# Late right-hand operands of a seven-product output projection loaded whole, row splits in one piece, and sums on GpSimd

## The chip, the cores and the metric

The kernel runs on one core of a Trainium2 chip. The metric is the time of one execution in microseconds (us), as the device reports it; lower is better. The kernel before the change took 889.74 us (median of three runs, 889.66 to 891.19).

A core has five engines with instruction queues of their own: TensorE (PE) multiplies matrices, VectorE (DVE) and ScalarE (ACT) work on rows of 128 partitions, GpSimd (POOL) and SyncE (SP) mostly issue DMAs. Each engine works through its queue in order, so an instruction that waits holds all that stand behind it on the same engine. DMAs are issued from the queues of SP, ACT and POOL.

## What is computed

The reference is one decoder block on 512 tokens of width 1024. Two mixers run on the normed input (a gated linear attention and a state-space layer), are merged by gates, projected by `w_out`, normed and added to the input; then a squared-ReLU feed-forward layer (FFN) with norms ahead of it and behind.

```python
mixed = jax.nn.sigmoid(z_gla) * y_gla + jax.nn.sigmoid(z_ssm) * y_ssm
h = h + rmsnorm(mixed @ w_out[l], g_mix_post[l])
hn = rmsnorm(h, g_ffn_pre[l])
f = jnp.square(jax.nn.relu(hn @ w_ff1[l])) @ w_ff2[l]
h = h + rmsnorm(f, g_ffn_post[l])
```

All is float32. `rmsnorm(x, g)` is `x * rsqrt(mean(x*x) + 1e-6) * g`.

## The kernel before

One function, `hybrid_block`, holds the whole block; 13,462 instructions. A float32 matrix is split into a high part (`hi`, rounded by ACT in `split_hi`, L160) and a low part (`lo = x - hi`, by VectorE), and a product of two matrices is three matmuls: hi·hi, hi·lo and lo·hi (in the names: `whi`, `wlo`, `hh`, `hl`, `gh`, `gl`, `bh`, `bl`). The order on each engine is made by a scheduler from the code and from hints: `with tc.issue_after(x)` puts what it holds behind instruction `x` in the order.

**Gated stage** (L1409 to L1489). The state-space output is loaded as eight tiles `qi` in POOL's queue (L1417) and split into `gh` and `gl`; products with `w_glu` give gate and value, two tiles of each in every one of four rounds (`c4`). In each round `out_load` (L1425) brings two 128-row blocks of `w_out` (1 MB, tile `woraw`, POOL's queue), and `out_weights` (L1430) makes from them a part of the operands of the output projection: three of the right-hand operands are split at once (`b1`, `b2_`, `b5_`), three sums `t2`, `t3`, `t4` are stored to device memory (`tdo`). `mixed` (L1443) makes the left-hand operands `ah`, `al` from the mixture tile `ms`.

**Output projection** (L1509 to L1629). The 512 x 1024 result is formed as a 2 x 2 block product by seven products instead of eight, on sums of blocks, named A11, A12, S1, S2, S4, S3, A22 in the order in which they run. Each (`out_product`, L1520) covers two token tiles `t` of 128 rows with 4 k-blocks of three matmuls 128x512: 12 matmuls to a tile, 24 to a product, summed in the PSUM banks `Xo`, `Yo`, `Zo`. The four late right-hand operands are b6 (for S2), b3 (S4), b7 (S3) and b4 (A22). `later_b` (L1527) fetches each in two loads of 512 KB from SP's queue into `wraw`, a ring of three buffers that the FFN's weights use too, and splits it in two pieces of 128x1024.

While products run, results of the finished ones are put together to rows: `out_half` (L1552) takes the squares of a half row tile on ACT and multiplies by `gpost`; `h_rows` (L1558) takes the root (`root`, L133: a Sqrt on ACT, small steps on VectorE, L140 to L147), adds the input rows `xt`, stores `h` (POOL's queue, L1567), takes the second root and scales the rows to `hn`. Rows 0 and 1 (the tiles with `t < 2`) come from the first products; rows 2 and 3 need A22. `turn_rows` (L1573) transposes `hn` by eight TensorE transposes for a row tile and splits it into `hh` and `hl`, a 128x128 piece at a time, multiplying by the gain `g_ffn_pre`, which here stands by column in `vecs`.

**First FFN tiles** (L1631 to L1643). Four weight tiles of `w_ff1` (`ws`; the fourth is `kept_w`) are multiplied with the first 256 tokens of `hh` and `hl` (24 matmuls 128x256 to a tile); the turns of rows 2 and 3 stand between them in PE's queue. After them come the second halves and the rest of the FFN.

Of the kernel before, what the change touches and what calls it, by code (L numbers as in the profile page):

```python
# [10 lines left out]
F32R = mybir.dt.float32r  # L11
# [6 lines left out]
P = 128  # L18
D = 1024
# [31 lines left out]
def hybrid_block(ctx: ExitStack, tc: tile.TileContext, io, out: bass.AP):  # L51
# [74 lines left out]
    vecs = mk(cst, [P, 44], tag="vecs")  # L126
    V_GN, V_BGLU, V_BGATE, V_D, V_GF = 0, 8, 24, 28, 36
# [31 lines left out]
    def split_hi(dst, src, scale=1.0):  # L159
        S.activation(dst, src, AF.Copy, scale=scale)  # L160
# [1251 lines left out]
    for m in range(KT):  # L1412
        if m == NBLK - 1:
            q = blocks[m].qT
        else:
            q = mk(pgl, [P, SEQ], tag="qi", bufs=4)
            nc.gpsimd.dma_start(q, qd[m])  # L1417
        split_hi(gh[:, m], q)
        V.tensor_sub(gl[:, m], q, f32(gh)[:, m])  # L1419

    def split_to(hi, lo, src):
        split_hi(hi, src)
        return V.tensor_sub(lo, src, f32(hi))  # L1423
# [36 lines left out]
    for c4, c in enumerate(range(0, D, 256)):  # L1460
        ss_ = []
        for i, w in enumerate(load_w(wg[:, D + c : D + c + 256])):
            m = c // P + i
            ps = bank("mm")
            feat_tile(w, gh, gl, 0, SEQ, ps)
            s_ = mk(pgl, [P, SEQ], tag="ms", bufs=2)
            S.activation(s_, ps, AF.Sigmoid, bias=vecs[:, V_BGLU + 8 + m : V_BGLU + 9 + m])
            zt = mk(pgl, [P, SEQ], tag="zi", bufs=2)
            nc.sync.dma_start(zt, zs[m])
            gated = V.tensor_mul(s_, s_, zt)  # L1470
            ss_.append(s_)
        with tc.issue_after(gated.ins):
            raw = out_load(c4)
            if c4 == 3:
                out_weights(c4, raw)
        for i, w in enumerate(load_w(wg[:, c : c + 256])):
            m = c // P + i
            ps = bank("mm")
            feat_tile(w, gh, gl, 0, SEQ, ps)
            t = mk(pgl, [P, SEQ], tag="ti", bufs=2)  # L1480
            nc.sync.dma_start(t, td[m])
            V.scalar_tensor_tensor(ss_[i], ps, vecs[:, V_BGLU + m : V_BGLU + m + 1], ss_[i], op0=ALU.add, op1=ALU.mult)
            added = V.tensor_add(ss_[i], ss_[i], t)
            mixed.even = ss_[0].rearrange("p (h t) -> p h t", h=2)
            mixed(c4, i, ss_[i])
        if c4 < 3:
            with tc.issue_after(added.ins):
                out_weights(c4, raw)
# [20 lines left out]
    sf = ExitStack()  # L1509
    pf = pool("pf", stack=sf, side="right", padded=True)  # L1510
    hh = mk(pf, [P, KT, SEQ], F32R, tag="hh")
    hl = mk(pf, [P, KT, SEQ], F32R, tag="hl")
    spt = ExitStack()
    pt = pool("pt", stack=spt, side="right", padded=True)
    gpost = mk(pt, [P, D], tag="gpost")
    nc.scalar.dma_start(gpost, io["g_mix_post"][0].partition_broadcast(P))
    Yo, Xo = ([bank("mm") for _ in range(2)] for _ in range(2))
    Zo = [bank() for _ in range(2)]

    def out_product(acc, i, b, t, first=False):  # L1520

        ts_ = slice(t * P, (t + 1) * P)
        for k in range(4):
            for n, (x_, w_) in enumerate(((ah[i], b[0]), (ah[i], b[1]), (al[i], b[0]))):
                PE.matmul(acc[t], x_[:, k, ts_], w_[:, k], start=first and k == 0 and n == 0, stop=k == 3 and n == 2, skip_group_check=True)

    def later_b(src):  # L1527

        hi, lo = b_slot()
        for jj in range(2):  # L1530
            raw = mk(wp, [P, 2, 512], tag="wraw", bufs=3)
            nc.sync.dma_start(raw, src(jj))
            later_b.made = split_to(hi[:, 2 * jj : 2 * jj + 2], lo[:, 2 * jj : 2 * jj + 2], raw)
        return hi, lo

    def sums_of(i):
        return lambda jj: tdo[i, 2 * jj : 2 * jj + 2].rearrange("j p n -> p j n")

    w22_of = lambda jj: w_out.rearrange("(j k p) n -> k p j n", k=2, p=P)[1, :, 2 * jj : 2 * jj + 2, 512:]
# [7 lines left out]
    def rows_x(t):  # L1547
        xt = xts_[t] = mk(pt, [P, D], tag="xt", bufs=2)
        for i in range(2):
            nc.sync.dma_start(xt[i * CH : (i + 1) * CH], io["x"][0].rearrange("(c t) d -> t c d", t=T8)[2 * t + i])  # L1550

    def out_half(t, n, i, src=None):  # L1552
        dst = rows_[t][:, sides[n]]
        src = dst if src is None else src
        out_half.squared = squares(pt, accs[t], i, src)
        V.tensor_mul(dst, src, gpost[:, sides[n]])

    def h_rows(t):  # L1558
# [5 lines left out]
        for n in range(2):  # L1564
            V.scalar_tensor_tensor(ht[:, sides[n]], ht[:, sides[n]], rs, xt[:, sides[n]], op0=ALU.mult, op1=ALU.add)  # L1565
# [3 lines left out]
        h_rows.done = V.tensor_scalar(hn[:, :512], ht[:, :512], rs, None, op0=ALU.mult)  # L1569
        h_rows.scaled = S.activation(hn[:, 512:], ht[:, 512:], AF.Copy, scale=rs)  # L1570
        return hn

    def turn_rows(t):  # L1573

        col = slice(t * P, (t + 1) * P)
        for q in range(2):
            pv = turned_tokens(hns[t], P, q, "sm")
            for k in range(4):
                kk = 4 * q + k
                g = vecs[:, V_GF + kk : V_GF + kk + 1]  # L1580
                S.activation(hh[:, kk, col], pv[:, k], AF.Copy, scale=g)  # L1581
                V.scalar_tensor_tensor(hl[:, kk, col], pv[:, k], g, f32(hh)[:, kk, col], op0=ALU.mult, op1=ALU.subtract)  # L1582
# [8 lines left out]
    b6 = later_b(sums_of(0))  # L1591
# [5 lines left out]
    b3 = later_b(w22_of)  # L1597
    ws = load_w(w1[:, : 3 * P])
    rows_[2], rows_[3] = row_tile(), row_tile()
# [5 lines left out]
    b7 = later_b(sums_of(1))  # L1605
# [3 lines left out]
    b4 = later_b(sums_of(2))  # L1609
    for t in range(2):  # L1610
        out_product(Yo, S4, b3, t)
        with tc.issue_after(later_b.made.ins):
# [3 lines left out]
    second = h_rows.done, h_rows.scaled  # L1616
# [16 lines left out]
    kept_w = [t[:, :2].rearrange("p a (k n) -> p (a k) n", n=P) for t in b_slot()]  # L1633
    raw = raw_w(w1[:, 3 * P : EARLY * P])[1]
    with tc.issue_after(second[0].ins), tc.issue_after(second[1].ins):
        split_to(*kept_w, raw)
# [185 lines left out]
def laid_out(np, given):  # L1822
# [4 lines left out]
    rows = {"vecs": np.concatenate([a[n][0].reshape(-1, P) for n in ("gla_norm_g", "b_glu", "b_gate", "d_skip", "g_ffn_pre")]).T}  # L1827
# [13 lines left out]
_LAID = ["g_mix_pre", "g_ffn_pre", "w_gate_up", "gla_norm_g", "b_glu", "b_gate", "d_skip", "a_re", "a_im", "log_step", "b_re", "b_im", "c_re", "c_im"]  # L1841
_INS = [
    "x", "meta_tokens", "w_in", "w_o_gla", "w_glu", "w_out", "g_mix_post", "w_ff1", "w_ff2", "g_ffn_post",
# [21 lines left out]
```

## Time and profile before

| | before |
|---|---|
| Median of three runs | 889.74 us (889.66 to 891.19) |
| The profiled execution: its own time | 888.97 us |
| Its span in the trace | 887.3 us |
| Mean granted TensorE clock | 0.991 of full speed |
| DVE busy | 685.1 us (77%) |
| ACT busy | 464.4 us (52%) |
| POOL busy | 131.2 us (15%) |
| HBM traffic over the span | 210 GB/s |

One execution is profiled. In a timeline a row gives the start in us, the duration in us, the engine, the line of the kernel, the operation and `out<-in` with the tiles' names, shape and type; xN means N like it in a row, and square brackets hold the time that the engine stood idle before it, with what released it. In the list of waits a row names who waited, for whom, and then us in total, times, and the longest. In a table of windows the columns are the stretch, its length, the busy time and count of PE, PE's weight loads, DVE, ACT and POOL, the granted clock, the DMA share and GB/s. In a row of groups, busy time and the mean nanoseconds of one stand behind the bar. A DMA row ends with KB for each and us from issue to landing. A busy time is a share of the span; what a wait costs is read at the engine that bounds.

### The profile page before, as it was taken

The page shows a single profiled execution, that of the slowest core. Times are in us where ns is not written, and L with a number is a line of the kernel's source. Part 1 is how long each engine was busy: PE and PEld are TensorE (multiplying, and loading weights), DVE is VectorE, ACT ScalarE, POOL GpSimd, SP SyncE. Part 2 cuts the span into 40 slices and gives each one's busy share as a digit, 9 for nine tenths or more (in the row PEclk, how much of TensorE's full clock was granted, in tenths as well). Part 3 has the DMA queues.
Part 4 walks back from the last instruction along what each step waited for, and adds up shares of the span by engine and source line. Part 5 has one row for each costly group of instructions (what it writes and reads, how often), then busy time and mean ns, then how long its engine had stood idle before and what let it go on. Part 6 is the DMA issues. An engine that isn't in the chain of part 4 may idle for free.

```text
span 887.3 us, 13462 instructions
## 1 busy us (share of the span) xinstructions
PE 865.2 (98%) x4824; PEld 738.5 (83%) x4824; DVE 685.1 (77%) x1267; ACT 464.4 (52%) x813; POOL 131.2 (15%) x229
## 2 busy tenths in 40 slices
PE   9999999999999999999999968999999999999996
PEld 8998989898988888887888856988888888888885
DVE  7999889978778699764777768566766768688786
ACT  7676467666755455244444557533222236665763
POOL 1113112031212222240111000011211200000001
PEclk9999999999999999999999997999999999999999
DMA  9767777546365857676665764289999876865564
GB/s 316 237 219 226 203 150 175 160 114 183 104 161 135 263 142 195 194 221 226 194 221 176 227 194 160 61 315 319 309 313 344 298 277 213 295 196 191 168 211 143
DMA packets 169835, 187.41 MB, mean 211 GB/s; under 512 B 18296, under 2 KB 127000, under 8 KB 169768
## 3 DMA queue, kind: packets, MB, share of 16 engines
q1 hardware_dynamic: 147856, 115.95, 44.2%
q0 software_dynamic: 19792, 65.87, 21.6%
q10 hardware_dynamic: 2120, 4.72, 1.8%
q8 instruction: 38, 0.62, 0.3%
q14 instruction: 29, 0.24, 0.1%
HBM read 147.42 MB, written 39.09 MB: 210 GB/s over the span
## 4 chain that ended last, share of the span: by engine, by line
PE 49%; DVE 2%; ACT 2%; DMA 1%; issue 0%; DVEq 0%; ACTq 0%
PE mm L61 34%; PE sm L61 15%; DMA wraw<-tdo 1%; ACT junk L1498 1%; DVE bl L1423 0%; ACT bh L160 0%; PE sm L66 0%; DVE hl L1582 0%; DVE c L1786 0%; DVE aq L1565 0%; DVE c L1780 0%; ACT L143 0%; DVE wlo L175 0%; ACT hh L1581 0%; ACT whi L160 0%
## 5 line engine op out<-in xcount | busy, mean ns | idle before, releaser
L160 ACT ACTIVATE whi<-wraw 128x1024 fp32r<-128x1024 f32 x81 | 85.8, 1060 | 191.1 <-PE mm L61 178.0
L175 DVE TENSOR_TENSOR wlo<-wraw,whi 128x1024 fp32r<-128x1024 f32 x81 | 98.6, 1223 | 83.4 <-ACT whi L160 83.1
L61 PE MATMUL mm<-xh,whi 128*128 128x512 f32 (+2 forms) x464 | 158.9, 342 | 0.0
L61 PE MATMUL mm<-xh,wlo 128*128 128x512 f32 (+2 forms) x464 | 155.8, 336 | 0.0
L61 PE MATMUL mm<-xl,whi 128*128 128x512 f32 (+2 forms) x464 | 155.6, 335 | 0.0
L61 PE MATMUL mm<-hl,whi 128*128 128x512 f32 (+1 forms) x272 | 102.2, 376 | 2.8 <-DVE hl L1582 1.5
L61 PE MATMUL mm<-hh,whi 128*128 128x512 f32 (+1 forms) x272 | 102.4, 377 | 1.0 <-ACT hh L1581 1.0
L61 PE MATMUL mm<-hh,wlo 128*128 128x512 f32 (+1 forms) x272 | 101.8, 374 | 0.0
L61 PEld LDWEIGHTS mm<-xh,whi 128*128 128x128 f32 x464 | 87.6, 189 | 9.6 <-issue 1.0
L61 PEld LDWEIGHTS mm<-xh,wlo 128*128 128x128 f32 x464 | 87.5, 189 | 9.0
L61 PEld LDWEIGHTS mm<-xl,whi 128*128 128x128 f32 x464 | 87.7, 189 | 8.4
L1723 DVE TENSOR_TENSOR wlo<-wraw,whi 128x1024 fp32r<-128x1024 f32 x56 | 68.4, 1223 | 20.0 <-ACT whi L1719 19.7
L61 PE MATMUL sm<-wlo,fh 128*128 128x512 f32 x192 | 74.8, 390 | 0.0
L61 PE MATMUL sm<-whi,fl 128*128 128x512 f32 x192 | 74.7, 389 | 0.0
L61 PE MATMUL sm<-whi,fh 128*128 128x512 f32 x192 | 74.7, 389 | 0.0
L1719 ACT ACTIVATE whi<-wraw 128x1024 fp32r<-128x1024 f32 x56 | 58.6, 1049 | 17.2 <-PE mm L61 11.7
L61 PEld LDWEIGHTS mm<-hl,whi 128*128 128x128 f32 x272 | 52.3, 192 | 12.4 <-DVE hl L1582 2.2
L61 PEld LDWEIGHTS mm<-hh,whi 128*128 128x128 f32 x272 | 52.4, 193 | 10.5 <-ACT hh L1581 1.7
L61 PEld LDWEIGHTS mm<-hh,wlo 128*128 128x128 f32 x272 | 52.3, 192 | 8.8
L160 ACT ACTIVATE fh<-f 128x512 fp32r<-128x512 f32 x48 | 30.3, 631 | 44.1 <-PE sm L61 30.2
L61 PE MATMUL mm<-gl,whi 128*128 128x512 f32 x128 | 50.0, 391 | 1.4 <-DVE gl L1419 1.4
L61 PE MATMUL mm<-gh,whi 128*128 128x512 f32 x128 | 50.0, 391 | 0.0
(474 smaller groups left out, 1861.9 us busy)
## 6 DMA issues: line engine op xcount, KB each, us to landing
wraw<-in_w_ff_dram SPq DMA_DIRECT2D x56, 512.0 KB, 4.8
wraw<-in_w_in_dram SPq DMA_DIRECT2D x46, 512.0 KB, 4.2
w2raw<-in_w_ff_dram POOLq DMA_DIRECT2D x16, 1024.0 KB, 8.8
t2d<-w2t POOLq DMA_DIRECT2D x16, 1024.0 KB, 5.8
wraw<-t2d SPq DMA_DIRECT2D x32, 512.0 KB, 3.7
wraw<-in_w_glu_dram SPq DMA_DIRECT2D x16, 512.0 KB, 6.3
M<-kpad POOLq DMA_DIRECT2D x64, 64.0 KB, 3.1
wraw<-in_w_o_gla_dram SPq DMA_DIRECT2D x8, 512.0 KB, 6.2
```

The costliest lines, as they stand in the source:

```text
L61: ins = nc.tensor.matmul(*args, **kw)
L160: S.activation(dst, src, AF.Copy, scale=scale)
L175: V.tensor_sub(lo, raw, f32(hi))
L1498: return S.activation(junk, src, AF.Square, accum_out=acc[:, i : i + 1])
L1719: halved = S.activation(bh, raw, AF.Copy)
L1723: V.tensor_sub(bl, raw, f32(bh))
```

## The change

- **Late operands.** The four raw right-hand operands (128x4x512, 1 MB each) are loaded whole (`raw_b`) from POOL's queue into a pool `pr`, which takes the memory in which `hh` and `hl` lie later; `later_b` only splits them, in two pieces as before. The input rows of `t < 2` are loaded in POOL's queue behind them.
- **Row splits.** `g_ffn_pre` is loaded as a broadcast row (`gffn`, a second load in ACT's queue behind `gpost`) and multiplied into the rows ahead of their scaling, the first half on GpSimd and the second on VectorE. `turn_rows` then splits a half row tile in one piece on ACT (L160) and one on VectorE (L213).
- **GpSimd** takes the two sums with `p5o`, two multiplies by `gpost`, and the four first-half multiplies by `gffn`.
- **Order.** The first FFN weights are split within the end of the gated stage, the fourth ahead of the split of b4; a Sqrt on a scrap tile has the ACT table loaded behind the split of b3; the turn of row 1 is put inside A22's second tile; the first `woraw` load goes behind all `qi` loads.

In the code (cut):

```diff
-            nc.gpsimd.dma_start(q, qd[m])
+            last_q = nc.gpsimd.dma_start(q, qd[m])
...
-        with tc.issue_after(gated.ins):
+        with tc.issue_after(last_q.ins):
             raw = out_load(c4)
+        with tc.issue_after(gated.ins), tc.issue_after(opened.ins):
             if c4 == 3:
                 out_weights(c4, raw)
...
+    gffn = mk(pt, [P, D], tag="gffn")
     nc.scalar.dma_start(gpost, io["g_mix_post"][0].partition_broadcast(P))
+    nc.scalar.dma_start(gffn, io["g_ffn_pre"][0].partition_broadcast(P))
...
+    def raw_b(i, src):
+        raw = mk(pr, [P, 4, 512], tag=f"rawb{i}")
+        nc.gpsimd.dma_start(raw, src)
+        return raw
...
-    def later_b(src):
+    def later_b(raw):
         hi, lo = b_slot()
-        for jj in range(2):
-            raw = mk(wp, [P, 2, 512], tag="wraw", bufs=3)
-            nc.sync.dma_start(raw, src(jj))
-            later_b.made = split_to(hi[:, 2 * jj : 2 * jj + 2], lo[:, 2 * jj : 2 * jj + 2], raw)
+        for kk in (slice(0, 2), slice(2, 4)):
+            later_b.made = split_to(hi[:, kk], lo[:, kk], raw[:, kk])
...
-        V.tensor_mul(dst, src, gpost[:, sides[n]])
+        out_half.made = (engine or V).tensor_mul(dst, src, gpost[:, sides[n]])
...
+            (V if n else G).tensor_mul(hn[:, sides[n]], ht[:, sides[n]], gffn[:, sides[n]])
...
-        h_rows.done = V.tensor_scalar(hn[:, :512], ht[:, :512], rs, None, op0=ALU.mult)
-        h_rows.scaled = S.activation(hn[:, 512:], ht[:, 512:], AF.Copy, scale=rs)
+        V.tensor_scalar(hn[:, :512], hn[:, :512], rs, None, op0=ALU.mult)
+        S.activation(hn[:, 512:], hn[:, 512:], AF.Copy, scale=rs)
...
     def turn_rows(t):
...
-                S.activation(hh[:, kk, col], pv[:, k], AF.Copy, scale=g)
-                V.scalar_tensor_tensor(hl[:, kk, col], pv[:, k], g, f32(hh)[:, kk, col], op0=ALU.mult, op1=ALU.subtract)
+        transpose_tokens(hns[t], P, hh, hl, t * P, "sm")
...
+    with tc.issue_after(later_b.made[0].ins):
+        S.activation(warm, warm, AF.Sqrt)
+    b7 = later_b(raws_b[2])
+    kept_w = [mk(pw, [P, KT, P], F32R, tag="aq", bufs=14) for _ in range(2)]
+    with tc.issue_after(later_b.made[0].ins), tc.issue_after(later_b.made[1].ins):
+        kept_made = split_to(*kept_w, raw_w(w1[:, 3 * P : 4 * P])[1])
...
-        V.tensor_add(rows_[2 + t][:, sides[1]], rows_[2 + t][:, sides[1]], p5o[:, sides[t]])
-        out_half(2 + t, 1, 0)
+        G.tensor_add(rows_[2 + t][:, sides[1]], rows_[2 + t][:, sides[1]], p5o[:, sides[t]])
+        out_half(2 + t, 1, 0, engine=G)
...
-        out_product(Xo, A22, b4, t)
-        turn_rows(t)
+        out_product(Xo, A22, b4, t, within=(lambda: turn_rows(1)) if t else None)
+        if not t:
+            turn_rows(0)
```

The order that results on three engines follows, with the program's names (a number behind a name tells tiles of one name apart).

POOL's queue at the output projection, before the change; `tdo` is a stored sum, `hd` the stored rows `h`:

```order
L1441 DMA tdo_4751<-qi_5404 128x512
L1567 DMA hd_5509<-aq_5554 128x1024
L1567 DMA hd_5509<-aq_5556 128x1024
L1567 DMA hd_5509<-aq_5634 128x1024
L1567 DMA hd_5509<-aq_5635 128x1024
```

and after it, where `rawb_946` to `rawb_949` are the raw operands of b6, b3, b7 and b4, and `aq` and `hn` rows:

```order
L1440 DMA tdo_4751<-qi_5404 128x512
L1532 DMA rawb_946_5526<-tdo_4751 128x4x512
L1532 DMA rawb_947_5528<-in_w_out_dram 128x4x512
L1532 DMA rawb_948_5530<-tdo_4751 128x4x512
L1532 DMA rawb_949_5532<-tdo_4751 128x4x512
L1556 DMA xt_5588<-in_x_dram 64x1024 x2
L1556 DMA xt_5607<-in_x_dram 64x1024 x2
L1573 TENSOR_TENSOR hn_5739<-aq_5562,gffn_5517 128x512
L1574 DMA hd_5509<-aq_5562 128x1024
L1632 TENSOR_TENSOR aq_5634<-aq_5634,aq_5659 128x512
L1632 TENSOR_TENSOR aq_5671<-aq_5671,aq_5659 128x512
L1573 TENSOR_TENSOR hn_5786<-aq_5564,gffn_5517 128x512
```

Four operand loads and four loads of input rows have come in ahead of the row stores, and arithmetic stands between the stores.

ACT's queue from the last raw operands to the first root, before; `bh_5699` is the high part of b4, `junk` a square, `wo_r` a root:

```order
L1608 COPY aq_5556<-mm_5523 128x512
L160 ACTIVATE bh_5663<-wraw_5665 128x1024
L160 ACTIVATE bh_5663<-wraw_5669 128x1024
L160 ACTIVATE bh_5699<-wraw_5701 128x1024
L160 ACTIVATE bh_5699<-wraw_5705 128x1024
L1498 ACTIVATE junk_5722,woacc_5526<-aq_5554 128x512
L143 ACT_TABLE_LOAD
L143 ACTIVATE wo_r_5726<-woacc_5526,wo_r_5726 128x1
```

and after, where `bh_5702` is b4's and `aq_5669` the fourth FFN tile's high part:

```order
L1605 ACT_TABLE_LOAD
L1605 ACTIVATE warm_74<-warm_74 128x1
L160 ACTIVATE bh_5663<-rawb_948_5530 128x1024 x2
L160 ACTIVATE aq_5669<-wraw_5672 128x1024
L1613 COPY aq_5562<-mm_5522 128x512
L1613 COPY aq_5564<-mm_5523 128x512
L160 ACTIVATE bh_5702<-rawb_949_5532 128x1024 x2
L1498 ACTIVATE junk_5727,woacc_5534<-aq_5562 128x512
L143 ACTIVATE wo_r_5731<-woacc_5534,wo_r_5731 128x1
```

The table load has moved ahead of the splits of b7, and a split of the fourth FFN tile has come in.

DVE's queue at the end of the gated stage, before; `ms` is a mixture tile, `aq_4732` and those behind it are left-hand operands:

```order
L1482 SCALAR_TENSOR_TENSOR ms_5364<-mm_5430,vecs_86,ms_5364 128x512
L1483 TENSOR_TENSOR ms_5364<-ms_5364,ti_5455 128x512
L1423 TENSOR_TENSOR aq_4732<-ms_5364,aq_4731 128x256
L1482 SCALAR_TENSOR_TENSOR ms_5394<-mm_5461,vecs_86,ms_5394 128x512
L1483 TENSOR_TENSOR ms_5394<-ms_5394,ti_5486 128x512
L1423 TENSOR_TENSOR aq_4734<-ms_5394,aq_4733 128x256
```

and after, with `wlo` the low parts of FFN weights:

```order
L1482 SCALAR_TENSOR_TENSOR ms_5364<-mm_5430,vecs_86,ms_5364 128x512
L175 TENSOR_TENSOR wlo_5626<-wraw_5622,whi_5624 128x1024
L1483 TENSOR_TENSOR ms_5364<-ms_5364,ti_5455 128x512
L1422 TENSOR_TENSOR aq_4732<-ms_5364,aq_4731 128x256
L1482 SCALAR_TENSOR_TENSOR ms_5394<-mm_5461,vecs_86,ms_5394 128x512
L1483 TENSOR_TENSOR ms_5394<-ms_5394,ti_5486 128x512
L175 TENSOR_TENSOR wlo_5632<-wraw_5628,whi_5630 128x1024
L1422 TENSOR_TENSOR aq_4734<-ms_5394,aq_4733 128x256
```

Two splits of FFN weights now stand ahead of left-hand operands.

More of the change, by code (lines that the diff above doesn't have):

```diff
@@ L1421, in split_to @@
     def split_to(hi, lo, src):
-        split_hi(hi, src)
-        return V.tensor_sub(lo, src, f32(hi))
+        return split_hi(hi, src), V.tensor_sub(lo, src, f32(hi))
     def out_load(j):
@@ L1486, in hybrid_block @@
         if c4 < 3:
-            with tc.issue_after(added.ins):
+            with tc.issue_after(added.ins), tc.issue_after(opened.ins):
                 out_weights(c4, raw)
@@ L1608, in hybrid_block @@
         S.copy(rows_[t][:, sides[1]], Xo[t])
-    b4 = later_b(sums_of(2))
+    with tc.issue_after(kept_made[0].ins), tc.issue_after(kept_made[1].ins):
+        b4 = later_b(raws_b[3])
+    spr.close()
+    sf = ExitStack()
+    pf = pool("pf", stack=sf, side="right", padded=True)
+    hh = mk(pf, [P, KT, SEQ], F32R, tag="hh")
+    hl = mk(pf, [P, KT, SEQ], F32R, tag="hl")
     for t in range(2):
         out_product(Yo, S4, b3, t)
-        with tc.issue_after(later_b.made.ins):
+        with tc.issue_after(out_half.made.ins):
             V.tensor_add(rows_[t][:, sides[1]], rows_[t][:, sides[1]], Yo[t])
@@ L1632, in hybrid_block @@
     w2 = io["w_ff2"][0]
[L1633 to L1636, printed above, removed]
     ws.append(kept_w)
```

49 lines of the change are left out of this document (21 added, 28 removed).

## The prediction

> **What bounds the kernel now.** I read the page's table of engines first, then PE's waits, then PE's timeline where the longest of them lies.
>
> ```profile
> span 887.3 us, 13462 instructions
> PE 865.2 (98%) x4824; PEld 738.5 (83%) x4824; DVE 685.1 (77%) x1267; ACT 464.4 (52%) x813; POOL 131.2 (15%) x229
> ...
> PE mm L61 <- ACT aq L1620: 7.2, 1, 7.2
> PE mm L61 <- DVE hl L1582: 1.5, 2, 1.0
> PE mm L61 <- DVE gl L1419: 1.4, 2, 1.2
> PE mm L61 <- DVE hn_r L140: 1.3, 1, 1.3
> PE mm L61 <- ACT hh L1581: 1.0, 3, 0.4
> ```
>
> TensorE is busy 865.2 of 887.3 us, so only some 22 us of waits and the stretches at a low clock can be won. The waits are few: one of 7.2 us on the copy at L1620, 3.8 us in sum on the turned rows (L1582, L1581, and the chain behind L140), 1.4 us on gl at the start of the gated stage. The change touches just these. PE's timeline gives the stage its frame:
>
> ```profile
> 492.08 0.39 PE L61 MATMUL mm<-bh,aq 128*128 128x512 f32 x1
> ...
> 524.49 0.39 PE L61 MATMUL mm<-bh,aq 128*128 128x512 f32 x1
> 532.09 0.80 PE L61 MATMUL mm<-bh,aq 128*128 128x512 f32 x1 [7.21 <-ACT aq L1620]
> ...
> 537.13 1.04 PE L66 MATMUL sm<-ident,hn 128*128 128x128 f32 x8
> 537.92 0.47 PE L61 MATMUL mm<-bh,aq 128*128 128x512 f32 x1
> ...
> 549.20 0.41 PE L61 MATMUL mm<-hh,wlo 128*128 128x256 f32 x1
> 553.89 0.29 PE L61 MATMUL mm<-hh,whi 128*128 128x256 f32 x1
> 554.02 0.27 PE L61 MATMUL mm<-hl,whi 128*128 128x256 f32 x1
> ...
> 563.04 0.28 PE L61 MATMUL mm<-hh,bl 128*128 128x256 f32 x1
> ```
>
> The first six products (144 matmuls) run from 492.08 to 524.72: 0.227 us each, 2.72 us for one product on one tile of 128 rows, 5.44 for both. From 524.72 to the end of the four early FFN tiles (563.16, one step of 0.12 after the last row) 38.4 us pass. Undisturbed the same work takes 5.4 (A22) + 4 x 0.79 (eight transposes, 537.13 to 537.92) + 96 x 0.119 (the rows from 553.89 on) = 20.0 us. **So 18.4 us are lost there**: 7.4 before A22; 2.3 as its first half takes 5.04 us (532.09 to 537.13) instead of 2.72; about 3.8 in waits on turned rows; 2.1 as the 22 matmuls from 549.20 to 553.89 take 0.213 us each; the rest in restarts.
>
> **What the 7.2 us are.** ACT's timeline, then VectorE's:
>
> ```profile
> 522.39 1.06 ACT L160 ACTIVATE bh<-wraw 128x1024 fp32r<-128x1024 f32 x1 [1.63 <-DMA wraw<-tdo]
> 526.14 1.28 ACT L143 ACT_TABLE_LOAD   x1
> 531.47 1.04 ACT L1620 COPY aq<-mm 128x512 f32<-128x512 f32 x2
> ...
> 523.48 1.23 DVE L1423 TENSOR_TENSOR bl<-wraw,bh 128x1024 fp32r<-128x1024 f32 x1 [1.46 <-ACT bh L160]
> 524.63 1.28 DVE L1613 TENSOR_TENSOR aq<-aq,mm 128x512 f32<-128x512 f32 x2
> 528.41 1.42 DVE L1565 SCALAR_TENSOR_TENSOR aq<-aq,wors,xt 128x512 f32<-128x512 f32 x2
> 534.09 1.41 DVE L1565 SCALAR_TENSOR_TENSOR aq<-aq,wors,xt 128x512 f32<-128x512 f32 x2
> 553.09 0.48 DVE L1569 TENSOR_SCALAR hn<-aq,hnrs 128x512 f32<-128x512 f32 x1
> ```
>
> The last right-hand operand lands at 522.4. VectorE adds the rows (L1613) only behind its split, at 524.63, though the products were there long before. From that add to the end of the first copy (531.47 + 0.55 = 532.05) the chain of squares, roots and copies takes 7.4 us, 1.28 of it a table load.
>
> **The change, part by part.** (1) *Operands.* They now come as four 1 MB loads in POOL's queue. The first waits for PE's last gated product (492.08), the other three for VectorE's last read of the mixture.
>
> ```profile
> 498.11 0.42 DVE L1423 TENSOR_TENSOR aq<-ms,aq 128x256 fp32r<-128x256 f32 x1
> ...
> w2raw<-in_w_ff_dram POOLq DMA_DIRECT2D x16, 1024.0 KB, 8.8
> ...
> 576.00:586.00 10.00, 10.00 (x46) 8.29 (x45) 7.83 (x12) 2.71 (x5) 0.58 (x2) 1.00 0.88 303
> ```
>
> That read ends at 498.5, and near 499.7 with the splits put ahead of it (3). Then 3 x 1.05 MB and two broadcast vectors of 0.5 MB are 4.2 MB. No row shows three such loads in one queue. At the 303 GB/s of the window they take 13.8 us (landed 513.5); at the rate of the w2raw row, two megabytes in flight per 8.8 us (238 GB/s), 17.6 us, and issue and latency put 2 us on that (519.5). I take 516, nearer to the window's rate, since there too several queues are at work. The first load has until S2 (492.08 + 72 x 0.227 = 508.4) and is not late by either rate; the x rows, 1 MB more behind the four, come 3.5 us later, near 519.5, and are wanted at 523. Behind it stand the two ACT pieces (1.06 each, the second VectorE piece trails by one), so the add of row tile 0 begins at 516 + 1.1 + 1.2 + 1.2 = 519.5, 5.1 us earlier than now. The fourth FFN tile's split (1.06 on ACT, 1.23 on VectorE) now stands ahead of these pieces and is covered by the wait for the load; without that cover it would cost its 1.2 us.
>
> (2) *The chain from that add.* It loses the table load (1.28; ACT waits on DMA just before, so its new place is covered) and gains 0.6 (the add of row tile 1 now stands between its reciprocal and its next step) and 0.3 (gain multiply ahead of L140): 7.4 - 1.3 + 0.9 = 7.0. The copy ends at 526.5, the PE is there at 524.7: **a stall of 1.9 us instead of 7.4.** With the early landing it is 0, with the late one 5.5.
>
> (3) *Cover for the FFN splits.* Two splits of 1.23 us now stand in VectorE's queue ahead of the last left operands. Today those of A11 are ready at 492.6 and read first at 492.08 + 9 x 0.227 = 494.1 (low half 494.6).
>
> ```profile
> 492.18 0.43 DVE L1423 TENSOR_TENSOR aq<-ms,aq 128x256 fp32r<-128x256 f32 x1 [0.48 <-ACT aq L160]
> 480.08 0.72 POOL L1427 DMA_DIRECT2D woraw<-in_w_out_dram  x1
> DMA to landing us min/median/max: 5.3/5.9/10.2
> 497.77 0.35 ACTq L1516 DMA_DIRECT2D gpost<-in_g_mix_post_dram  x1
> ```
>
> At 1.23 later they still meet the low half with 0.8 us left. The weights are now issued beside the woraw load of 480.08; if they land like the slowest of that tile's answer (10.2 us) and not like its median (5.9), near 492 that is, VectorE stands up to 2 us and A11 with it. gpost is issued about 2 us later than now and holds VectorE at L1562, ahead of the first late operand's split. For both I reserve 0.9 us, between 0 and 1.8.
>
> (4) *The rows' turns.* The gain sits in hn beforehand, so a half is split by one ACT and one DVE piece of 128x512 (0.63 us, 0.68) in place of four of each (0.35 each). Row tile 0: hn is scaled some 2.6 us after its root's Sqrt, near 528.1, inside A22's first tile (526.5 to 529.3): hidden. Row tile 1 stands 5.7 us behind in the rows of L1565 now; without the two sums between (1.35, now on GpSimd) and with the multiply (0.6) 5.0, so it is scaled near 532.6; PE wants it after turn 0 and six matmuls, at 531.5: stall 1.1. Then A22 ends near 534.9; the first FFN tile waits 0.8 for its split; turn 2 waits 0.3. Row tile 3 is scaled 12.8 us after A22's end today (L1569 at 553.09 and 0.48, against 537.92 + 12 x 0.227 = 540.6); fewer pieces in between, the fourth FFN tile's split (1.06 and 1.23) among those that go, make it about 12, near 546.9, and PE is there at 544.6: stall 2.3. Waits in all: 1.9 + 1.1 + 0.8 + 0.3 + 2.3 = 6.4.
>
> (5) *The clock.* After 7.2 us the clock is halved, but also after waits on turned rows of 1.3 us at most:
>
> ```profile
> 545.00:550.00 5.00, 3.25 (x11) 2.25 (x12) 4.68 (x21) 4.08 (x14) 0.53 (x1) 0.71 0.46 166
> 550.00:555.00 5.00, 5.00 (x30) 5.00 (x29) 2.79 (x9) 2.40 (x6) 0.53 (x1) 0.61 0.26 105
> ```
>
> The new waits are as long as these but farther apart; each low stretch costs 2.1 to 2.3. I take 0.8 in all (bounds 0 and 4.4), and 0.9 for restarts. [...]
>
> So 6.4 + 0.8 + 0.9 = 8.1 stands where 18.4 stood: **the stage gains 10.3.**
>
> (6) *Start of the gated stage.* All qi loads now go ahead of woraw on POOL.
>
> ```profile
> 406.08 0.50 PE L61 MATMUL mm<-gl,whi 128*128 128x512 f32 x1 [0.23 <-DVE gl L1419]
> 408.53 0.50 PE L61 MATMUL mm<-gl,whi 128*128 128x512 f32 x1 [1.21 <-DVE gl L1419]
> 398.62 1.60 POOL L1417 DMA_DIRECT2D qi<-qd  x3
> ```
>
> The last three are issued at 398.6, behind woraw and td; two of them move up, the last one doesn't pass td. Of 1.4 us I take 0.8 (0 to 1.4).
>
> (7) *GpSimd* gets eight operations of two 128x512 inputs: four gain multiplies, two sums, two multiplies.
>
> ```profile
> L306 POOL TENSOR_SCALAR_AFFINE_SELECT sc<-sc 128x512 f32<-128x512 f32 x1 | 0.6, 633 | 0.0
> L305 POOL MEMSET sc<- 128x512 f32 x1 | 0.5, 531 | 0.1
> L160 ACT ACTIVATE fh<-f 128x512 fp32r<-128x512 f32 x48 | 30.3, 631 | 44.1 <-PE sm L61 30.2
> L175 DVE TENSOR_TENSOR wlo<-wraw,whi 128x1024 fp32r<-128x1024 f32 x81 | 98.6, 1223 | 83.4 <-ACT whi L160 83.1
> ```
>
> No two-input one is in the trace. One input takes 0.63; I take twice that, 1.3, with 0.6 (half a VectorE piece of L175, two inputs) as the lower bound; no row bounds it from above, so the upper end is where it decides. The eight and four store issues (0.7 each, as the woraw row) run in series from the first row's L1571 (523.5) until row tile 3 needs the last, at about 544: up to (544 - 523.5 - 2.8) / 8 = 2.2 us each, they hide behind VectorE's and ACT's own chain. VectorE loses eight pieces of 0.69, which the 12 us of (4) hold already.
>
> **Sum.** 10.3 + 0.8 - 0.9 = 10.2 from the profiled execution's 888.97 gives 878.8. That execution lies 0.77 under the median of 889.74, so the forecast is **879.5**.
>
> **Rivals.** *Operands late and clock down:* landing at 519.5 makes A22 wait 5.5 (3.6 more), and a wait that long halves the clock as the 7.2 did (1.5 more than taken): 884.6, with a spread to 886. For it speak the w2raw row and queue order, against it the window's 303. Chance 0.22. *Everything hides:* landing at 513.5, no clock lost, no reserve: 1.9 + 0.8 + 0.9 off, near 875.9; chance 0.11. *VectorE held by GpSimd:* if a GpSimd operation holds a two-input one of VectorE for its whole length, once in each of the three turns on the path, 3 x 1.3 = 3.9 more: 883.4. The trace has no such pair, so nothing speaks for or against; chance 0.06. [...] *It doesn't do what it says:* the operands land when they land now, since the queue was full, and the rows' chain stays late; only small terms move, 889; chance 0.06. *Slower:* GpSimd becomes the bound. Its queue ends at 526.3 + 8d, and 6.8 us of scaling, turning and matmuls follow (2.5 + 0.8 + 3.5); this passes today's 563.16 at d = 3.8. At 4.2 us the end is 566.7, 3.5 later than now, less the 0.8 of the start: 892.4. It needs over six times the one-input row, and no row shows such a factor. Chance 0.07.
>
> **How the numbers follow.** The forecast, 877 to 882.5 by its own smaller terms, has 0.48; the rivals 0.22, 0.11, 0.06, 0.06 and 0.07. Range 875.5 to 886: it takes in the two landing bounds. Faster by over 0.2% (1.8 us, about what a measurement of this kernel can tell): 0.48 + 0.22 + 0.11 + 0.06 = 0.87; same 0.06; slower 0.07.
>
> **What would show it.** Right: PE's wait on the copy of Xo falls from 7.2 to about 2 (0 to 5.5); the rawb loads land by 516; no table load behind L1624; the waits on gl at 406 to 409 shrink; GpSimd's operations take 0.6 to 2.2 us. Wrong: a new wait of A11 on a left operand near 494, of S2 on bl near 508, S4's or S3's operands late, a PE wait whose releaser is POOL, or a PEclk row that is lower through the FFN tiles than now.

## The result and the profile after

The changed kernel takes **879.66 us** (median of four runs, 879.35 to 880.48) against 890.37 us for the kernel before on the same chip (four runs): a ratio of 0.9881 with a 95% interval of 0.9864 to 0.9898, so 1.2% faster, 10.7 us. The profiled execution took 879.52 us, its span 877.6 us. Run again later, the same kernel gave 0.9885 (0.9861 to 0.9910).

The forecast was 879.5. The total agrees to 0.2 us, but its terms don't: some were too small, others too large, and they cancel. That is the subject of the rest.

The head of the page of the changed kernel, and then its list of PE's waits, in the same columns as those of before:

```profile
span 877.6 us, 13428 instructions
PE 860.9 (98%) x4824; PEld 737.3 (84%) x4824; DVE 686.8 (78%) x1243; ACT 458.0 (52%) x790; POOL 147.8 (17%) x245
```

```profile
PE sm L66 <- DVE hn L1576: 5.4, 3, 4.0
PE mm L61 <- ACT aq L1630: 1.1, 1, 1.1
```

The 7.2 us on the copy of Xo are 1.1 now, the waits on gl at the gated stage's start are gone from the list, and so are those on hh and hl. A new line has come: 5.4 us on the scaled rows (L1576), 4.0 of them at one place. PE's timeline shows where (turn n is the transposing of row tile n, the rows with L66):

```profile
490.16 0.39 PE L61 MATMUL mm<-bh,aq 128*128 128x512 f32 x1
...
522.58 0.39 PE L61 MATMUL mm<-bh,aq 128*128 128x512 f32 x1
524.07 0.50 PE L61 MATMUL mm<-bh,aq 128*128 128x512 f32 x1 [1.10 <-ACT aq L1630]
...
527.30 1.09 PE L66 MATMUL sm<-ident,hn 128*128 128x128 f32 x8 [0.22 <-DVE hn L1576]
...
533.84 1.97 PE L66 MATMUL sm<-ident,hn 128*128 128x128 f32 x8 [4.04 <-DVE hn L1576]
535.46 0.78 PE L61 MATMUL mm<-bh,aq 128*128 128x512 f32 x1
...
538.17 0.41 PE L61 MATMUL mm<-hh,whi 128*128 128x256 f32 x1
...
539.66 0.29 PE L61 MATMUL mm<-hl,whi 128*128 128x256 f32 x1
...
548.90 1.07 PE L66 MATMUL sm<-ident,hn 128*128 128x128 f32 x8 [1.13 <-DVE hn L1576]
...
553.27 0.28 PE L61 MATMUL mm<-hh,aq 128*128 128x256 f32 x1
```

A11 starts at 490.16 instead of 492.08. From the end of S3 (the row at 522.58 and 0.23, 522.81) to the end of the early FFN tiles (the row at 553.27 and 0.12, 553.39) 30.6 us pass, 7.9 less than the 38.4 before. Of these 10.6 are lost against the undisturbed 20.0: 6.5 in four waits (1.10, 0.22, 4.04, 1.13), 2.8 behind the longest of them at a low clock (0.53 granted in 535 to 540; the turn takes 1.62 us instead of 0.79, six matmuls 2.71 instead of 1.36, seven of the FFN 1.49 instead of 0.83), the rest in restarts.

What makes row 1 late stands in VectorE's timeline, beside GpSimd's:

```profile
516.48 0.68 DVE L1624 TENSOR_TENSOR aq<-aq,mm 128x512 f32<-128x512 f32 x1
...
521.23 1.68 DVE L1573 TENSOR_TENSOR hn<-aq,gffn 128x512 f32<-128x512 f32 x1
...
524.06 1.35 DVE L146 SCALAR_TENSOR_TENSOR hn_r<-hnrs,hn_r 128x1 f32<-128x1 f32 x1
525.33 0.15 DVE L145 RECIPROCAL wors<-wo_r 128x1 f32<-128x1 f32 x1
525.44 1.21 DVE L147 SCALAR_TENSOR_TENSOR hnrs<-hn_r,hnrs 128x1 f32<-128x1 f32 x1
...
528.80 1.67 DVE L1573 TENSOR_TENSOR hn<-aq,gffn 128x512 f32<-128x512 f32 x1
...
530.95 0.16 DVE L145 RECIPROCAL hnrs<-hn_r 128x1 f32<-128x1 f32 x1
531.15 1.84 DVE L146 SCALAR_TENSOR_TENSOR hn_r<-hnrs,hn_r 128x1 f32<-128x1 f32 x1
...
533.30 0.48 DVE L1576 TENSOR_SCALAR hn<-hn,hnrs 128x512 f32<-128x512 f32 x1
```

```profile
520.62 1.74 POOL L1573 TENSOR_TENSOR hn<-aq,gffn 128x512 f32<-128x512 f32 x1 [17.70 <-DVE aq L1571]
...
524.10 2.53 POOL L1632 TENSOR_TENSOR aq<-aq,aq 128x512 f32<-128x512 f32 x2 [1.20 <-ACT aq L1630]
528.18 1.74 POOL L1573 TENSOR_TENSOR hn<-aq,gffn 128x512 f32<-128x512 f32 x1 [1.55 <-DVE aq L1571]
...
530.49 2.49 POOL L1562 TENSOR_TENSOR aq<-aq,gpost 128x512 f32<-128x512 f32 x2
```

A step on 128x1 numbers (L146) takes 1.35 and 1.84 us and ends with GpSimd's operation (525.4; 532.99 against GpSimd's 532.98, the end of the second of two that follow each other); undisturbed it takes 0.22. The reciprocal beside it, with one input, takes its usual 0.15. The lengthened instructions on the way to row 1 are L1573 (1.68 and 1.67 instead of 0.69), L146 (1.35, 1.84) and L147 (1.21 instead of 0.16): 5.8 us in all.

Not each part of the gain is steady. From the first product of the gated stage to A11 the changed kernel takes 87.04 us in this execution, and so do eight of the experiments below that keep its order of loads; in e10, where it was run again, it takes 88.24, with short waits on gh (0.41) and gl (0.22).

### The profile page after: what moved, and what is told of

Its sections match the earlier page's. It is cut to its first block, busy times and chain, and to the rows that moved or that the text cites. A ratio compares the mean times of both kernels' runs of the same rounds, so it can differ in the third digit from the quotient of the medians.

```text
span 877.6 us, 13428 instructions
## 1 busy us (share of the span) xinstructions
PE 860.9 (98%) x4824; PEld 737.3 (84%) x4824; DVE 686.8 (78%) x1243; ACT 458.0 (52%) x790; POOL 147.8 (17%) x245
## 4 chain that ended last, share of the span: by engine, by line
PE 83%; DVE 6%; issue 5%; DMA 3%; ACT 2%; POOL 0%; ACTq 0%; DVEq 0%; POOLq 0%
PE mm L61 59%; PE sm L61 22%; PE sm L66 2%; DMA wraw<-in_w_in_dram 1%; DMA rawb<-in_w_out_dram 1%; DMA b<-bd 1%; ACT bh L160 1%; DVE wlo L79 0%; DVE M L79 0%; DVE bl L1422 0%; DVE hn_r L146 0%; DVE hn L1573 0%; DMA tdo<-qi 0%; DVE aq L1571 0%; DVE c L1793 0%
## 5 line engine op out<-in xcount | busy, mean ns | idle before, releaser
L160 ACT ACTIVATE whi<-wraw 128x1024 fp32r<-128x1024 f32 x81 | 85.8, 1059 | 192.3 <-PE mm L61 178.5
L160 ACT ACTIVATE fh<-f 128x512 fp32r<-128x512 f32 x48 | 30.3, 631 | 44.4 <-PE sm L61 30.6
L61 PE MATMUL mm<-gh,wlo 128*128 128x512 f32 x128 | 49.8, 389 | 0.0
```

Of the source, the lines that this page charges most:

```text
L61: ins = nc.tensor.matmul(*args, **kw)
L160: return S.activation(dst, src, AF.Copy, scale=scale)
```

## The experiments

All times are medians of four or five runs; a ratio is against the kernel before, run between them on the same chip. The experiments ran in three groups, each on one chip. Times of different groups differ by some tenths, so where runs of different groups are set side by side, the ratios decide.

**Who holds VectorE.** Four kernels, the first group. The first takes all eight operations from GpSimd:

```diff
-            (V if n else G).tensor_mul(hn[:, sides[n]], ht[:, sides[n]], gffn[:, sides[n]])
+            V.tensor_mul(hn[:, sides[n]], ht[:, sides[n]], gffn[:, sides[n]])
...
-        G.tensor_add(rows_[2 + t][:, sides[1]], rows_[2 + t][:, sides[1]], p5o[:, sides[t]])
-        out_half(2 + t, 1, 0, engine=G)
+        V.tensor_add(rows_[2 + t][:, sides[1]], rows_[2 + t][:, sides[1]], p5o[:, sides[t]])
+        out_half(2 + t, 1, 0)
```

> The changed kernel with GpSimd's eight operations (two sums, two multiplies by gpost, four by gffn) back on VectorE, all else as changed. Theory (holds): a VectorE instruction with two tensor inputs stands still while a GpSimd one runs; in the changed trace this lengthens L1573 from 0.69 to 1.7 and L146 and L147 from 0.2 to 1.2-1.8, some 5.8 us on the way to row tile 1. Then VectorE's extra work (eight times 0.6) costs less than the holds: PE's wait ahead of the turn of row 1 falls from 4.0 to 1-2 us and the time to 876.5-878.5. Rival (relief): GpSimd's work is a real relief of a busy VectorE, and putting it back costs 2-4 us: 881.5-884, with the wait at 5 us or more.

Measured 876.72 us (0.9839, 0.9817 to 0.9860), 3.7 us faster than the changed kernel by the ratios (2.9 by the medians), though VectorE has eight pieces more. L146 and L147 are back at 0.22 and 0.16 us, and L1573 at 0.69 (mean of the group 685 ns). The wait ahead of turn 1, however, is 3.28 us, not 1 to 2:

```profile
531.43 1.88 PE L66 MATMUL sm<-ident,hn 128*128 128x128 f32 x8 [3.28 <-DVE hn L1576]
```

VectorE's own share explains it (the columns of the windows are as before; the third number with a count is DVE's):

```profile
520.00:525.00 5.00, 4.77 (x21) 3.65 (x20) 4.89 (x18) 4.01 (x11) 0.57 (x1) 1.00 0.52 141
525.00:530.00 5.00, 3.15 (x18) 2.34 (x17) 5.00 (x13) 3.86 (x13) 0.54 (x1) 1.00 0.55 154
```

VectorE is busy 9.89 of 10 us: with the holds gone it is itself the bound there; e9 below bears this out. So relief would be welcome; GpSimd's does not relieve.

The second kernel leaves GpSimd's work and rewrites the two small steps so that they have one tensor input:

```diff
-        V.scalar_tensor_tensor(a, y, hm, y, op0=ALU.mult, op1=ALU.mult)
-        return V.scalar_tensor_tensor(y, a, 1.5, y, op0=ALU.add, op1=ALU.mult)
+        V.tensor_scalar(a, y, hm, y, op0=ALU.mult, op1=ALU.mult)
+        return V.tensor_scalar(y, a, 1.5, y, op0=ALU.add, op1=ALU.mult)
```

> The changed kernel with the root's two small steps (L146, L147) written with one tensor input and the other factor as a per-partition scalar; GpSimd keeps all eight operations. Theory (holds by two-input instructions only): L146 and L147 take 0.2 us even while a GpSimd operation runs; some 3.8 us go from the way to row tile 1, PE's wait ahead of its turn falls from 4.0 to 0.5-1.5 us, time 876-877.5. Rival (any VectorE instruction, or only those on small tiles, slows beside GpSimd; or they wait for something else): L146 and L147 stay above 1 us and the time stays at 879-880.

Measured 879.76 us (0.9872, 0.9848 to 0.9895): no gain, although L146 and L147 do what the theory says. VectorE's timeline (the profiled execution is the slowest of the four):

```profile
525.65 0.27 DVE L146 TENSOR_SCALAR hn_r<-hnrs,hn_r 128x1 f32<-128x1 f32 x1
...
525.96 0.21 DVE L147 TENSOR_SCALAR hnrs<-hn_r,hnrs 128x1 f32<-128x1 f32 x1
...
526.28 0.99 DVE L1576 TENSOR_SCALAR hn<-hn,hnrs 128x512 f32<-128x512 f32 x1
...
527.42 2.20 DVE L1571 SCALAR_TENSOR_TENSOR aq<-aq,wors,xt 128x512 f32<-128x512 f32 x2
...
532.01 0.27 DVE L146 TENSOR_SCALAR hn_r<-hnrs,hn_r 128x1 f32<-128x1 f32 x1
...
532.64 1.50 DVE L1576 TENSOR_SCALAR hn<-hn,hnrs 128x512 f32<-128x512 f32 x1
```

L146 and L147 no longer wait while GpSimd runs (its two sums lie at 525.69 to 528.41 in this run, its two multiplies at 531.35 to 533.85), as the theory has it. But the next instructions run into the same operations: L1576 takes 0.99 and 1.50 instead of 0.49, L1571 2.20 for two instead of 1.41. The first part of the theory, "two-input instructions only", is refuted by L1576, which has one tensor input. In this run the wait ahead of turn 1 is 3.26 us, and the waits ahead of A22 (1.93) and turn 3 (2.13) are longer than in the changed kernel. VectorE reached the next wide instruction earlier, and that one waited. This doesn't account for all of it: row 0's add stands 0.7 us later behind A11's start here than in the changed kernel, as does VectorE's split of the last operand ahead of it (24.8 us behind that start instead of 24.1), and the longer wait ahead of A22 comes of that; and ahead of turn 3 the unaltered kernel itself waits 1.90 in e10. Why the median shows no gain at all is in part open.

Side by side: where a GpSimd operation ran, the two-input L146 took 1.84 us against 0.22 (changed kernel), and the `tensor_scalar` of 128x512 (L1576) 1.50 against 0.49 (here); the `tensor_scalar` steps of 128x1 (0.27 and 0.21) showed no delay. What in the chip makes the difference was not shown.

The third and the fourth split the eight operations into the four multiplies by gffn and the rest, with the corresponding lines of the first diff:

> The changed kernel with only the four first-half multiplies by gffn (L1573) back on VectorE; sums and gpost multiplies stay on GpSimd. Theory (holds): the two halves run in series on VectorE at 0.6-0.7 each, 1.3 together, less than the 1.7 that one takes beside GpSimd's: 0.4 us won for each row tile, 1 us in all, 878-879.3; L146 and L147 are still held by the sums. Rival (relief): 1-2 us lost, 880.5-882.

> The changed kernel with the two sums and the two multiplies by gpost back on VectorE; the four multiplies by gffn stay on GpSimd. Theory (holds): L146 and L147 go back to 0.2 us (3.8 us won on the way to row tile 1), four VectorE pieces of 0.6 come in (2.4, of them 1.2 ahead of row tile 1's root): PE's wait ahead of the turn of row 1 is 1.5-3 us, time 877-879. Rival (relief): 881-882.

With the multiplies by gffn back on VectorE: 878.84 us (0.9859, 0.9837 to 0.9880), inside the expected range, the wait ahead of turn 1 still 3.98. With the sums and gpost multiplies back: 876.76 us (0.9838, 0.9816 to 0.9860), 0.2 us under the expected 877 to 879; the wait is 3.44, a little over the expected 3. The intervals of the third and the changed kernel overlap, so its gain (0.8 us by the medians, 2.0 by the ratios) is a tendency; the fourth's interval ends at 0.9860, just below where the changed kernel's begins. It alone gives what the first gives: the price lies in the two sums and two multiplies that run beside the roots.

**The other parts, one by one.** Four kernels, the second group, each undoing one part of the change. First the order of the gated stage's loads:

```diff
-        with tc.issue_after(last_q.ins):
+        with tc.issue_after(gated.ins):
             raw = out_load(c4)
```

> The changed kernel with the first woraw load again behind the first round's gates only, so that it can go ahead of the last qi loads, all else as changed. Theory (the trace's account): the gated stage was shortened by 2.5 us (from its first gl product to A11 89.6 us before, 87.0 after), waits of 1.4 us on gl and the restarts behind them; undoing it gives 881.5-882.8. Rival (the prediction's term): 0.8 us, 880.2-880.8.

Measured 883.33 us (0.9910, 0.9891 to 0.9929), above both ranges, and spread from 881.3 to 885.3. That is 2.6 us more than the changed kernel by the ratios, whose intervals overlap, and 3.7 more than e7 of the same group, whose slowest run (881.22) lies below the fastest here (881.32). The waits on gl are back (0.23 and 1.22), with 0.49 on gh ahead of them:

```profile
410.91 0.50 PE L61 MATMUL mm<-gl,whi 128*128 128x512 f32 x1 [1.22 <-DVE gl L1419]
```

In the profiled execution, the slowest of the five, the clock then falls to 0.67 in 410 to 415, and from the first product to A11 91.7 us pass. The rival's 0.8 us is too small; how much more than that this part is worth differs between executions.

Then the operands, in halves from SP's queue through `wraw`:

```diff
-        raw = mk(pr, [P, 4, 512], tag=f"rawb{i}")
-        nc.gpsimd.dma_start(raw, src)
-        return raw
+        return src
...
+            part = mk(wp, [P, 2, 512], tag="wraw", bufs=3)
+            nc.sync.dma_start(part, raw[:, kk])
-            later_b.made = split_to(hi[:, kk], lo[:, kk], raw[:, kk])
+            later_b.made = split_to(hi[:, kk], lo[:, kk], part)
```

> The changed kernel with the four late operands loaded as before, in halves of 512 KB from SP's queue through the ring of three wraw buffers, all else as changed. Theory (the loads set the rows): the last operand is split near 522 again, PE's wait on the copy of Xo ahead of A22 is 5-7 us, the clock is halved behind it, 886-889. Rival (the early FFN weights free the ring, so half loads come in time as well): wait under 2.5 us, 879.5-881.5.

Measured 884.17 us (0.9924, 0.9907 to 0.9940), 2 us below the theory's range but far from the rival's. Its mechanism is there: the last operand's second half is split on ACT at 522.97, 8.8 us later than in the changed kernel (the second of two pieces from 513.11, 1.0 behind), PE waits 5.66 us for the copy of Xo and then runs at half clock. Row 0's add itself is no later (516.48 in both); in this order the splits of the late halves stand between that add and the rows' next steps, so that L1571 begins 7.0 us behind the add instead of 3.3. In the windows of e6, PE's busy time stands first and the granted clock third from the end:

```profile
525.00:530.00 5.00, 0.71 (x2) 0.62 (x3) 4.54 (x12) 2.66 (x8) 2.74 (x3) 0.77 0.85 236
530.00:535.00 5.00, 5.00 (x16) 3.84 (x15) 4.93 (x7) 2.59 (x7) 3.65 (x4) 0.54 0.49 182
```

One reason that the size is smaller than expected is that A22's later start leaves only 1.87 us of the wait ahead of turn 1; ahead of turn 3 PE waits 2.57.

The table load (the Sqrt on the scrap tile left out):

> The changed kernel without the Sqrt on the scrap tile, so that the ACT table is loaded behind the first squares of row tile 0, all else as changed. Theory: the 1.28 us stand in the chain of all rows: the wait ahead of A22 goes from 1.1 to 2.4 us, the wait ahead of turn 1 stays, 880.6-881.2. Rival (the load is hidden by the wait for VectorE): no change, 879.4-880.

Measured 879.66 us (0.9873, 0.9854 to 0.9893): nothing. In the time the rival is right. The load stands in the chain in ACT's timeline,

```profile
516.81 0.63 ACT L1498 ACTIVATE junk<-aq 128x512 f32<-128x512 f32 x1 [2.08 <-DVE aq L1622]
...
517.55 1.28 ACT L143 ACT_TABLE_LOAD   x1
518.84 0.29 ACT L143 ACTIVATE wo_r<-woacc,wo_r 128x1 f32<-128x1 f32 x1
```

but VectorE's order has changed with it: the add of row tile 1 (0.68) stands ahead of the reciprocal there and fills the time. From row 0's add to its L1571 it takes 3.73 us with the load and 3.31 without; the remaining 0.4 is made up by an earlier add (25.8 us behind A11's start instead of 26.3). That has a reason too. ACT's timeline in the changed kernel, and below it in e7:

```profile
505.43 2.01 ACT L160 ACTIVATE bh<-rawb 128x1024 fp32r<-128x1024 f32 x2 [0.82 <-DMA rawb<-in_w_out_dram]
...
507.92 1.28 ACT L1605 ACT_TABLE_LOAD   x1
...
513.11 2.01 ACT L160 ACTIVATE bh<-rawb 128x1024 fp32r<-128x1024 f32 x2
```

```profile
506.00 2.01 ACT L160 ACTIVATE bh<-rawb 128x1024 fp32r<-128x1024 f32 x2 [1.28 <-DMA rawb<-in_w_out_dram]
...
512.72 2.01 ACT L160 ACTIVATE bh<-rawb 128x1024 fp32r<-128x1024 f32 x2
```

From the second operand's landing to the split of b4 ACT works without a pause in the changed kernel, and the load lies in that stretch: 7.68 us with it, 6.72 without. So its early place isn't free either.

The turn of row 1 behind A22's second tile:

```diff
-        out_product(Xo, A22, b4, t, within=(lambda: turn_rows(1)) if t else None)
-        if not t:
-            turn_rows(0)
+        out_product(Xo, A22, b4, t, within=None)
+        turn_rows(t)
```

> The changed kernel with the turn of row 1 behind A22's second tile instead of within it, all else as changed. Theory (a wait halves the clock when it is long enough; those of up to 3.3 us in the runs so far left most of it, that of 4.0 halved it for 5.8 us): the six matmuls fill 1.4 us of the wait, the rest of 2.7 us leaves the clock at full, and some 3 us are won: 876-877.5. Rival (the place within A22 hides the split of the turned rows): the first FFN tile waits 0.8-1.2 us more and the clock is as before, 880-881.

Measured 880.93 us (0.9883, 0.9866 to 0.9900), as the rival said: the wait ahead of the turn is 2.72 us, as expected, but 0.94 us follow on the split, and the clock falls all the same (0.58 and 0.74 in the two stretches of 5 us from 535 to 545):

```profile
534.64 1.10 PE L66 MATMUL sm<-ident,hn 128*128 128x128 f32 x8 [2.72 <-DVE hn L1576]
536.67 0.58 PE L61 MATMUL mm<-hh,whi 128*128 128x256 f32 x1 [0.94 <-ACT hh L160]
```

The theory of a limit on the single wait fails.

**A better version.** VectorE was the bound in e1, and four pieces there belong to rows 2 and 3. They go behind row 1 (cut; `h_rows.done` and `h_rows.scaled` are the scaling of a row tile's two halves):

```diff
+    row1 = h_rows.done, h_rows.scaled
...
+        with tc.issue_after(row1[0].ins), tc.issue_after(row1[1].ins):
+            V.tensor_add(rows_[2 + t][:, sides[1]], rows_[2 + t][:, sides[1]], p5o[:, sides[t]])
+            out_half(2 + t, 1, 0)
```

> The kernel of e1 (all eight operations on VectorE) with the two sums of rows 2 and 3 and their squares and gpost multiplies put behind the scaling of row tile 1 in the order. Theory (in e1 VectorE itself is the bound on the way to row tile 1: it is busy 5.0 of 5.0 us, and four pieces of 0.6 there belong to rows 2 and 3): PE's wait ahead of turn 1 falls from 3.3 to about 1 us, the clock stays up, 873-875. Rival (the pieces only move: rows 2 and 3 come later by as much and PE waits there instead): the waits ahead of turns 2 and 3 grow by 1.5-2.5 us, 876-877.5.

> The changed kernel itself, unaltered, to have it beside e9 on the same chip: 879-880.5 by either theory, PE's wait ahead of turn 1 near 4.0 us, L146 and L147 at 1.2-1.8 us where a GpSimd operation runs.

In the third group: 875.88 us (0.9834, 0.9815 to 0.9852) against 880.33 us (0.9885, 0.9861 to 0.9910) for the changed kernel, so 4.4 us better than the change and the fastest of all. The time lies between the two expected ranges, and both accounts hold in part. The wait ahead of turn 1 falls to 1.25 us (4.05 in e10) and the clock stays at 1.00 throughout this stage, but PE now waits 0.96 ahead of turn 2 and 1.85 ahead of turn 3 (none and 1.10 in e1). PE's row in e9, the windows of e9, and below them one of the changed kernel:

```profile
529.61 1.10 PE L66 MATMUL sm<-ident,hn 128*128 128x128 f32 x8 [1.25 <-DVE hn L1576]
```

```profile
525.00:530.00 5.00, 3.75 (x23) 2.92 (x22) 4.93 (x14) 3.26 (x8) 0.54 (x1) 1.00 0.74 238
530.00:535.00 5.00, 4.42 (x32) 3.96 (x31) 4.75 (x16) 3.18 (x9) 0.00 (x0) 1.00 0.19 67
535.00:540.00 5.00, 4.04 (x35) 3.87 (x34) 4.92 (x17) 3.17 (x9) 0.53 (x1) 1.00 0.26 105
```

```profile
535.00:540.00 5.00, 5.00 (x20) 4.42 (x19) 4.93 (x11) 3.20 (x10) 1.72 (x2) 0.53 0.00 0
```

VectorE is as busy in both (4.92 and 4.93 of 5), but the clock is at 1.00 and at 0.53. Against e1 the gain is 0.8 us between different groups, which is not more than a tendency.

## Why the prediction came out right, point by point

- **Operands and the wait ahead of A22 (predicted 1.9 us, measured 1.3).** Right in the main, and the runs show it: in halves again, the operands cost 4.5 us (e6 at 884.17 against 879.66, e7's time in the same group; 3.8 against the changed kernel by the ratios). Landing was put at 516; the four loads landed within 11.4 us of their issue, so by 511.5, as the queues moved 402 GB/s in 505 to 510, more than the 303 used. The 2 us for issue and latency in the late landing were the author's estimate; no run shows a latency alone (issuing one of the four took 0.75 us, and in the kernel before a 256 KB store `tdo` took 2.3 us from issue to landing, its data included). The rows' add begins 26.3 us behind A11's start (predicted 27.4), but not for the reason given. The prediction let the last landing set it; ACT took the last operand up 1.6 us after it was there, as it had been busy since the second operand came at 505.43. In all nine profiled executions with whole loads and the early table load, the add stands 11.05 to 11.08 us behind the start of that operand's split, whatever else was altered. The chain behind the add is 7.5 us long, not 7.0: L1573, held by GpSimd, delays the root.
- **The table load (predicted -1.28 in the chain).** Its removal was worth nothing measurable (e7), since the add of row 1 takes its place: the prediction charged that add as 0.6 in the chain with the load gone, and didn't see that the add would have hidden half the load. It also took the load's new place as covered, since ACT waits on a DMA just before; that wait ends ahead of the load, and the load then lengthens ACT's way to the last operand by 1.0 (7.68 against 6.72 us).
- **Cover for the FFN splits and gpost (reserve 0.9, measured 0).** VectorE did stand 2.03 us on gpost, at 501, but nothing late came of it.
- **Turn of row 1 (predicted 1.1, measured 4.04).** This step failed. "VectorE held by GpSimd" stood in the text as a rival with a chance of 0.06 and a price of 3.9 us; it is what happened, at this turn above all, and the rows of e1, e2 and e4 show the holds. The step took a GpSimd operation for relief at its own duration (1.3 predicted, 1.27 measured at L1562) and priced only its lateness, not the other engine's. How much the holds cost is seen from row 0's add to row 1 scaled. The prediction had 13.1 us there (519.5 to 532.6). Measured are 17.3 in the changed kernel, 15.1 in e1, where no hold is left but all eight pieces are on VectorE, and 13.1 in e9, where the four pieces of rows 2 and 3 stand behind row 1 as well. So the forecast's way was right for a row 1 that meets neither, and taking the holds away alone brings back only half of the 4.2 us; PE's wait falls by 0.8 in e1, as A22 starts earlier as well.
- **The other turns (predicted 0.8 + 0.3 + 2.3, measured 0 + 0 + 1.1, and 0.2 at turn 0).** Too high, so that the waits come to 6.5 in sum where 6.4 was forecast; the longer wait at turn 1 gave rows 2 and 3 the time, as e9 shows from the other side.
- **The clock (predicted 0.8, measured 2.8).** The term's size hung on turn 1: in e9, with 1.25 us there, the clock stays up (1.00 from 520 to 550).
- **Start of the gated stage (predicted 0.8, at most 1.4; measured 2.5).** The step took the listed waits on gl for the whole loss. From the first product with gh to A11 89.57 us passed before (402.51 to 492.08) and 87.04 after (403.12 to 490.16), and 384 matmuls at 0.227 are 87.2: the loss was 2.5, of which the list of waits names 1.4. The same subtraction was made for the FFN tiles and not here. e5 speaks for at least this size; in e10, though, 1.2 of it is lost again in the unaltered kernel.
- **The sum.** 7.9 us from the end of S3 to the end of the early FFN tiles instead of 10.3, 2.5 at the start of the gated stage instead of 0.8, no reserve of 0.9, and 0.7 lost in stretches that were not part of the sum (0.6 ahead of the gated stage, 0.1 behind the early FFN tiles): 9.7 between the spans, 9.4 between the profiled executions, where 10.2 was forecast. Two errors of some 2 us with opposite signs and several smaller ones met; the forecast's accuracy is luck. That the late operands were the largest cost is not luck, though the way by which they set the rows was another.

## What to carry to other kernels

Work moved to GpSimd was not free for VectorE here: instructions with two SBUF inputs, and the `tensor_scalar` of 128x512, took up to 1.1 us longer where they met one operation of 1.3 to 1.7 us (L1573 1.68 us instead of 0.69, L147 1.21 instead of 0.16, L1576 of e2 1.50 instead of 0.49), and L146, where two operations follow each other, 1.84 instead of 0.22. So price such work at its own duration on each VectorE instruction of these forms that may meet it, above all on small steps of a chain that others wait for; here 12 us of GpSimd work (6.8, 2.5 and 2.5) made the kernel 3 to 4 us slower than the same work on VectorE, eight pieces of 0.7. Ask also which pieces need to stand ahead of the row that is waited for: e9 got the forecast's way by order alone. Where an engine's waits are read from a list, check their sum against the undisturbed time of the stage; restarts and the clock don't stand in it. And where a load is taken out of a chain, ask first which work the scheduler would put in its place, and whether the engine is really idle where the load goes.

## What the runs showed of the hardware

- VectorE instructions with two SBUF inputs stood until GpSimd's operation ended, even on 128x1 (L146 in the changed kernel: 1.84 us instead of 0.22, across the end of one operation and the whole of the next); a `tensor_scalar` of 128x512 was held too (L1576 in e2: 1.50 instead of 0.49), one of 128x1 (L146 in e2: 0.27) and a reciprocal (L145 in the changed kernel: 0.15) weren't.
- GpSimd's multiply at L1573 took 1.69 us (mean of four in the changed kernel), issued while VectorE's L1571 ran, and the one at L1562 1.27. Whether VectorE holds GpSimd in turn was not shown, since no run had L1573 on GpSimd without L1571 beside it.
- In the two cases seen, an instruction with one of its inputs in PSUM was not held: in e4 L213 ran 0.68 us at 536.63, within GpSimd's 536.23 to 537.87, and in e2 0.69 us at 544.59, within 544.20 to 545.84.
- The clock: it stayed at full (1.00) after single waits of 1.10 us (changed kernel, 525 to 530), 1.93 and 3.26 (e2, 525 to 530 and 535 to 540). It was about halved for some 5 to 6 us after waits of 4.04 (changed kernel, 0.53 in 535 to 540), 5.66 (e6, 0.54 in 530 to 535) and 7.2 (kernel before, 0.50 in 530 to 535). After 3.28 and 3.44 us it fell for some 3 us (e1 and e4, 0.66 and 0.74 in 530 to 535), and after 2.72 and 0.94 in short succession for 5 (e8, 0.58 and 0.74 in 535 to 545). In e2 the matmuls of 128x256 behind a wait of 2.13 us stood 0.21 us apart instead of 0.12, from 549.7 to 552.9; in the kernel before, whose waits from 537 to 549 were no longer than 1.3 us, the clock was at 0.71 and 0.61 in 545 to 555. So the length of the single wait does not decide it alone: 3.26 us left the clock up, 2.13 did not. What decides was not shown.
